# Attention block: weights' lower parts on GpSimd in halves, one reciprocal for two rows, output halves stored apart and added on reload

## The chip, the cores and the metric

The kernel runs on one core of one Trainium2 chip. The metric is the device time of one execution in microseconds. Five engines work side by side, each through its own instruction stream in a fixed order: TensorE (PE; its weight loads are PEld), VectorE (DVE), ScalarE (ACT), GpSimd (POOL) and SyncE (SP), which issues nearly all DMA transfers. An engine that waits for an input holds up everything behind it in its own stream.

## The reference

One decoder layer, 1024 tokens, width 1024. The input is normalised and multiplied by `w_in`. From the columns of that product come a forgetting attention ("fox", 8 heads of 64, causal, with a cumulated log-sigmoid bias), a sparse attention ("nsa", 8 heads of 64 in two key/value groups) and two gates. Cut to what matters here:

```python
z = h @ w_in
p = softmax(q_i k^T * SCALE + c_i - c_j)              # fox, causal
o_fox = p @ v
p_cmp, p_slc, p_win = softmax of compressed, selected, window scores
o_nsa = g0 * (p_cmp @ vc) + g1 * (p_slc @ v_sel) + g2 * (p_win @ vw)
merged = sigmoid(g_a) * (o_fox @ w_br_fox) + sigmoid(g_b) * (o_nsa @ w_br_nsa)
x = x + merged @ w_out
x = x + square(relu(rms(x) @ w_ff1)) @ w_ff2
return rms_norm(x, g_final)
```

The softmax of each row needs its exponentials, their sum (the denominator), the reciprocal of the sum, and a multiplication of the row by it.

## The kernel before

**Two-part numbers.** A matrix product is computed in three passes of rounded operands: a tensor is kept as an upper part (`hi`, a rounded copy) and a lower part (`lo`, the tensor less its rounded copy), and the product is hi·hi + hi·lo + lo·hi. For every weight tile of 128x1024, `wsplit` makes the upper part with a cast on ScalarE (L206, `wh_...`) and the lower part with one subtraction on VectorE (L207, `wl_...`). Names: `fq`, `fk`, `fv` and `nq`, `nk`, `nv` are the projections of the two attentions, `kc`, `vc`, `w1kc`, `w1vc` belong to the compressed keys and values, `g_0` to `g_7` are the gates' weights, `brf` and `brn` the two branch projections after the attentions.

**Stages of the trace.** Start and first projections (0 to 90 us), fox attention (90 to about 330), nsa attention (about 330 to 830), the nsa branch and `w_out` (830 to 960), the two feed-forward stages (960 to 1576).

**Order of the work.** `attend` writes the attention units out in turn. A unit is a pair of 128-row query blocks; for nsa it covers two heads. Between the attention's steps it puts steps of a feed: projections for later units, the gates, and at the end of the nsa stage the fox branch `brf`. The feed's pieces fill TensorE while the softmax runs on the other engines. A scheduler then fixes each engine's order from modelled times; attention steps have priority, so a feed step that is not ready in the model stands further back in TensorE's order.

**An attention unit.** Scores `sf`, `sn` are made on TensorE into three PSUM buffers; VectorE adds bias or mask and takes the minimum (L825); ScalarE takes the exponential with the sum as a by-product (L838, `denf`, `denn`); VectorE takes the reciprocal (L840, `rdf`, `rdn`); GpSimd multiplies the row (L841). Names end in the row block (0 to 7) and for nsa in `c`, `s` or `w`: compressed, selected, window; tile `pn` holds selected probabilities, `wn` compressed and window ones. TensorE transposes 128x128 blocks of a row into one of two PSUM buffers (`ptf`, `ptn`, L160); ScalarE casts them (L865 and L855) and VectorE subtracts for the lower part (the same lines); TensorE multiplies the transposed chunk with the values into `accs` (L157).

**Output of a unit.** `accs` holds, on 64 partitions, the product with the values' upper part, and on the other 64 that with the lower part. `finish` copies one half on ScalarE (L876), adds the other on VectorE (L877), each 64x256, and stores the sum to `of_d` or `on_d` in HBM. Two nsa units (`KEEP`) write straight to the tile `on`.

**Reload.** `load_of` brings the fox outputs back in eight pieces: a DMA into a buffer of the ring `vt` (L1386, `orof`), a cast on ScalarE (L1387) and a subtraction on GpSimd (L1388) into the tiles `of`. The ring `vt` has three buffers in the nsa stage (`VTN`), and is used too by the gates (`sg`: tanh on ScalarE, L786, scale on GpSimd, L787, store) and by six of the eight feature blocks of the fox branch (`msf`). `load_of` stands in the feed between the first and the second token halves of the last three gates (`g_5_0`, `g_6_0`, `g_7_0`, then the reload, then `g_5_1`, `g_6_1`, `g_7_1`), and before `brf`. The projections and gates share two PSUM buffers (`Pj`): a gate's buffer is free when its tanh has run. `load_on` does the same for the nsa outputs, placed inside the fox branch.

## Time and profile before

| | |
|---|---|
| three timed runs | 1580.92, 1578.37, 1581.56 us (median 1580.92) |
| span of the profiled execution, first to last instruction | 1576.0 us |
| mean granted TensorE clock | 0.999 |
| PE busy | 1560.9 us (99%), 7952 instructions |
| DVE busy | 1099.8 us (70%), 2434 instructions |
| ACT busy | 859.6 us (55%), 1604 instructions |
| POOL busy | 364.0 us (23%), 433 instructions |

The page gives the profiled execution only by its span; the three timed runs lie 2.4 to 5.6 us above it, which is taken as what lies around the span. Read it so: an instruction's duration runs from its start to its modelled end, and pipelined matmuls overlap, so eight matmuls of 128x512 in a row that "take 1.98 us" start their successor 1.81 us after their own start. A row of the timeline gives start, duration, engine, line, operation, output <- inputs, shape, count, and in brackets the idle time before it with what ended it.

### The profile page before, as it was taken

How to read it: one execution, taken by the hardware profiler on the slowest of the kernel's cores; microseconds unless marked ns; L12 is line 12 of the kernel's file. 1: busy time of each engine (PE TensorE's matmuls, PEld its weight loads, DVE VectorE, ACT ScalarE, POOL GpSimd, SP SyncE). 2: the span in 40 equal slices, each digit the busy share in tenths (PEclk: the TensorE clock that was granted, in tenths of full speed). 3: DMA queues.
4: the chain of work that ended last, by engine and by line, in shares of the span. 5: the costliest groups of instructions: out<-in, count | busy, mean ns of one | idle time of the engine just before them, and what ended most of it. 6: DMA issues, size and time to landing. Idle time of an engine off the chain costs nothing.

```text
span 1576.0 us, 23281 instructions
## 1 busy us (share of the span) xinstructions
PE 1560.9 (99%) x7952; PEld 1316.9 (84%) x7952; DVE 1099.8 (70%) x2434; ACT 859.6 (55%) x1604; POOL 364.0 (23%) x433
## 2 busy tenths in 40 slices
PE   8999999999999999999999999999999999999998
PEld 7888888888888888888888888888888888888886
DVE  7677768757566677548658389665556599777877
ACT  6666666646565676558543267555555644333335
POOL 1133333213332233236310000433333100000002
PEclk9999999999999999999999999999999999999999
DMA  6321212242222122224448552554444696545312
GB/s 192 77 59 49 65 49 63 90 109 64 64 74 68 34 54 74 62 68 135 156 162 299 190 167 87 194 169 155 157 148 147 224 324 217 159 145 169 112 54 107
DMA packets 165951, 196.66 MB, mean 125 GB/s; under 512 B 21497, under 2 KB 101433, under 8 KB 165825
## 3 DMA queue, kind: packets, MB, share of 16 engines
q1 hardware_dynamic: 165832, 195.18, 38.7%
q8 instruction: 63, 1.03, 0.3%
q14 instruction: 56, 0.45, 0.1%
HBM read 139.99 MB, written 55.15 MB: 124 GB/s over the span
## 4 chain that ended last, share of the span: by engine, by line
PE 94%; DVE 2%; ACT 1%; DMA 1%; SPq 1%; issue 0%; DVEq 0%; ACTq 0%
PE g L157 11%; PE fX L157 11%; PE oX L157 10%; PE accs L157 9%; PE fZ L157 6%; PE wo L157 5%; PE oZ L157 5%; PE ptn L160 4%; PE nq L157 3%; PE brn L157 3%; PE fk L157 3%; PE fv L157 3%; PE fq L157 3%; PE fW L157 2%; PE brf L157 2%; PE oW L157 2%
## 5 line engine op out<-in xcount | busy, mean ns | idle before, releaser
L157 PE MATMUL oX<-to,so 128*128 128x512 f32 x672 | 154.6, 389 | 0.0
L157 PEld LDWEIGHTS oX<-to,so 128*128 128x128 f32 x672 | 126.2, 188 | 26.2
L865 DVE TENSOR_TENSOR PTn<-ptn,PTn 128x512 fp32r<-128x512 f32 (+1 forms) x136 | 91.2, 672 | 67.8 <-ACT PTn L865 66.7
L1875 ACT CAST to<-w 128x1024 fp32r<-128x1024 f32 x48 | 48.2, 1051 | 146.8 <-PE accs L157 55.8
L865 ACT CAST PTn<-ptn 128x512 fp32r<-128x512 f32 (+1 forms) x136 | 76.6, 570 | 73.4 <-PE ptn L160 62.6
L157 PE MATMUL fX<-ht,w1h 128*128 128x512 f32 x384 | 95.0, 389 | 0.6 <-DVE ht L1581 0.6
L1713 POOL TENSOR_TENSOR ss<-w 128x512 f32<-128x512 f32 x14 | 22.4, 1602 | 309.6 <-DMA w<-in_w_ff_dram 189.0
L157 PE MATMUL accs<-PTn,Vnv 128*128 128x512 f32 (+1 forms) x304 | 92.4, 393 | 0.5 <-DVE PTn L865 0.5
L157 PEld LDWEIGHTS fX<-ht,w1h 128*128 128x128 f32 x384 | 72.0, 188 | 15.9 <-DVE ht L1581 1.0
L841 POOL TENSOR_SCALAR pf<-pf,rdf 128x896 f32<-128x896 f32 (+3 forms) x64 | 51.3, 807 | 141.9 <-DVE rdf L840 116.3
L1993 POOL TENSOR_TENSOR z<-x,gf 128x512 f32<-128x512 f32 x8 | 11.0, 1395 | 306.1 <-DVE x L1924 303.8
L157 PE MATMUL oZ<-to,so 128*128 128x512 f32 x336 | 77.6, 389 | 0.0
L157 PE MATMUL g<-hTh,wh_g 128*128 128x512 f32 (+1 forms) x288 | 76.3, 385 | 1.2 <-ACT hTh L311 1.2
L1703 DVE TENSOR_TENSOR w1l<-w,w1h 128x1024 fp32r<-128x1024 f32 (+1 forms) x32 | 34.6, 1081 | 60.4 <-ACT w1h L1702 60.4
L157 PE MATMUL g<-hTl,wh_g 128*128 128x512 f32 (+1 forms) x288 | 75.9, 384 | 0.1
L157 PEld LDWEIGHTS oZ<-to,so 128*128 128x128 f32 x336 | 63.1, 188 | 13.1
L157 PE MATMUL g<-hTh,wl_g 128*128 128x512 f32 x256 | 70.3, 396 | 0.0
L1876 DVE TENSOR_TENSOR so<-hr,so 128x1024 fp32r<-128x1024 f32 x56 | 68.0, 1236 | 0.9 <-ACT so L1875 0.9
L1875 ACT CAST so<-hr 128x1024 fp32r<-128x1024 f32 x56 | 56.7, 1049 | 18.2 <-DMA hr<-hid_d 18.1
L838 ACT ACTIVATE pf<-pf,mf 128x896 f32<-128x896 f32 (+3 forms) x64 | 49.7, 777 | 23.8 <-DVE mf L825 21.2
L1876 DVE TENSOR_TENSOR to<-w,to 128x1024 fp32r<-128x1024 f32 x48 | 56.7, 1220 | 7.7 <-ACT to L1875 7.7
L157 PEld LDWEIGHTS g<-hTh,wh_g 128*128 128x128 f32 x288 | 51.1, 188 | 10.8 <-ACT hTh L311 2.1
(511 smaller groups left out, 4248.8 us busy)
## 6 DMA issues: line engine op xcount, KB each, us to landing
w<-in_w_ff_dram SPq DMA_DIRECT2D x62, 512.0 KB, 4.4
hr<-hid_d SPq DMA_DIRECT2D x56, 512.0 KB, 4.5
wr_wo<-in_w_out_dram SPq DMA_DIRECT2D x20, 512.0 KB, 3.8
x<-in_x_dram SPq DMA_DIRECT2D x16, 512.0 KB, 8.8
wr_g<-in_w_in_dram SPq DMA_DIRECT2D x16, 512.0 KB, 3.8
hid_d<-h22s SPq DMA_DIRECT2D x32, 256.0 KB, 2.2
hid_d<-s2s SPq DMA_DIRECT2D x32, 256.0 KB, 2.0
hid_d<-s3h SPq DMA_DIRECT2D x32, 256.0 KB, 2.3
```

What stands on the lines that cost most here:

```text
L157: self.last = self.nc.tensor.matmul(*a, **k)
L160: self.last = self.nc.tensor.transpose(*a, **k)
L838: nc.scalar.activation(p, p, AF.Exp, bias=nm, scale=-1.0, accum_out=den)
L841: self.scaled = nc.gpsimd.tensor_scalar(p, p, r, 1.0 if gate is None else gate, op0=OP.mult, op1=OP.mult).ins
L865: two = nc.scalar.copy(th, src).ins, nc.vector.tensor_sub(tl, src, th.bitcast(F32)).ins
L1703: nc.vector.tensor_sub(lo, src, hi.bitcast(F32))
L1713: e.tensor_add(p[:, 4:8], b[:, 0:4], b[:, 4:8])
L1875: nc.scalar.copy(o[:, 0, s], src)
L1876: nc.vector.tensor_sub(o[:, 1, s], src, o[:, 0, s].bitcast(F32))
L1993: nc.gpsimd.tensor_mul(y[:, c], x[:, c], gf[:, c])
```

## The change

Four edits, all in the two attention stages:

1. `wsplit`: while `lo_pool` is set (both `attend` calls and what stands between them), the lower part of a weight tile is made by GpSimd in two subtractions of 128x512 instead of one of 128x1024 on VectorE. By the engines' orders these are 46 weight tiles: 92 instructions on GpSimd in place of 46 on VectorE. The `brn` and `wo` weights stay on VectorE.
2. `softmax`: the denominators of two rows stand side by side and share one reciprocal. In a fox unit these are the unit's two rows, and both rows' multiplications stand behind the second row's exponential; in nsa they are the compressed and the selected part of one row. 256 reciprocals become 160.
3. `finish`: `accs` is copied as it is by one ScalarE instruction (128x256 or 128x512) and both halves are stored apart, so VectorE's additions go and 46 stores become 92. The two `KEEP` units stay as they were.
4. `load_o`: each of the 16 reloads fetches two halves into two buffers of the ring `vt` and adds them on GpSimd (128x512) before the cast and the subtraction.

```diff
-            nc.vector.tensor_sub(lo, raw, hi.bitcast(F32))
+            if self.lo_pool:
+                k = shape[0] // 2
+                for c in (slice(0, k), slice(k, 2 * k)):
+                    nc.gpsimd.tensor_sub(lo[:, c], raw[:, c], hi[:, c].bitcast(F32))
+            else:
+                nc.vector.tensor_sub(lo, raw, hi.bitcast(F32))
...
-    def softmax(self, p, nm, name, gate=None):
+    def softmax(self, rows, name, box=None, last=True):
...
-        nc.scalar.activation(p, p, AF.Exp, bias=nm, scale=-1.0, accum_out=den)
-        r = sp.tile([P, 1], F32, tag="rd", bufs=8, name=f"rd{name}")
-        nc.vector.reciprocal(r, den)
-        self.scaled = nc.gpsimd.tensor_scalar(p, p, r, 1.0 if gate is None else gate,
-                                              op0=OP.mult, op1=OP.mult).ins
+        for p, nm, gate in rows:
+            n = len(box["rows"])
+            nc.scalar.activation(p, p, AF.Exp, bias=nm, scale=-1.0, accum_out=box["den"][:, n:n + 1])
+            box["rows"].append((p, gate))
+        if not last:
+            return
+        n = len(box["rows"])
+        r = sp.tile([P, 2], F32, tag="rd", bufs=8, name=f"rd{name}")
+        nc.vector.reciprocal(r[:, 0:n], box["den"][:, 0:n])
+        for x, (p, gate) in enumerate(box["rows"]):
+            self.scaled = nc.gpsimd.tensor_scalar(p, p, r[:, x:x + 1], 1.0 if gate is None else gate,
+                                                  op0=OP.mult, op1=OP.mult).ins
...
-        t = self.att.tile([P, 256], F32, tag="ot", bufs=3, name=f"ot{name}")
+        m = len(js)
+        t = self.att.tile([P, m, 256], F32, tag="ot", bufs=4 - m, name=f"ot{name}")
+        if dst is not None:
+            nc.scalar.copy(t, pa[:, 0:m * 256].rearrange("p (j q) -> p j q", j=m))
+            for x in range(2):
+                nc.sync.dma_start(dst[x].rearrange("(j d) t -> d j t", j=m)[:, :, q0:q0 + 256],
+                                  t[64 * x:64 * x + 64])
+            return
...
-                raw = self.att.tile([P, H], F32, tag="vt", bufs=self.VT, name=f"or{name}{half}{j}")
-                nc.sync.dma_start(raw[:, c], src[j * P:(j + 1) * P, half * H + c.start:half * H + c.stop])
+                raw, low = (self.att.tile([P, H], F32, tag="vt", bufs=self.VT, name=f"or{name}{half}{j}{x}")
+                            for x in range(2))
+                for x, d in enumerate((raw, low)):
+                    nc.sync.dma_start(d[:, c], src[x, j * P:(j + 1) * P, half * H + c.start:half * H + c.stop])
+                nc.gpsimd.tensor_add(raw[:, c], raw[:, c], low[:, c])
```

The edits also move instructions far from their own lines, since the scheduler orders by modelled times. Three places follow. In the changed kernel L841 is L858, L787 is L793, L207 is L210 on GpSimd, L1387 and L1388 are L1414 and L1415, and the new addition is L1413; a row ending in x2 stands for two such instructions.

GpSimd's order at the start of the fox reload, in the nsa stage. Before:

```order
L1388 TENSOR_TENSOR of_8660<-orof_8662,of_8660 128x512
L1388 TENSOR_TENSOR of_8661<-orof_8666,of_8661 128x512
L841 TENSOR_SCALAR wn_6_8647<-wn_6_8647,rdn_6c,gate 128x64
L1388 TENSOR_TENSOR of_8660<-orof_8670,of_8660 128x512
L1388 TENSOR_TENSOR of_8661<-orof_8674,of_8661 128x512
L841 TENSOR_SCALAR pn_6_8650<-pn_6_8650,rdn_6s,gate 128x896
L1388 TENSOR_TENSOR of_8660<-orof_8678,of_8660 128x512
```

And now:

```order
L1413 TENSOR_TENSOR orof_8429<-orof_8429,orof_8430 128x512
L1415 TENSOR_TENSOR of_8427<-orof_8429,of_8427 128x512
L1413 TENSOR_TENSOR orof_8436<-orof_8436,orof_8437 128x512
L858 TENSOR_SCALAR wn_6_8414<-wn_6_8414,rdn_6s,gate 128x64
L858 TENSOR_SCALAR pn_6_8417<-pn_6_8417,rdn_6s,gate 128x896
L1415 TENSOR_TENSOR of_8428<-orof_8436,of_8428 128x512
L1413 TENSOR_TENSOR orof_8443<-orof_8443,orof_8444 128x512
L210 TENSOR_TENSOR wl_brf_8354<-wr_brf_8112,wh_brf_8353 128x512 x2
L858 TENSOR_SCALAR wn_6_8414<-wn_6_8414,rdn_6w,gate 128x640
L1415 TENSOR_TENSOR of_8427<-orof_8443,of_8427 128x512
L1413 TENSOR_TENSOR orof_8450<-orof_8450,orof_8451 128x512
```

Each piece of the reload now has two GpSimd instructions, and the branch weights' lower parts stand between them, ahead of the probabilities' multiplications.

GpSimd's order at the end of the same reload, where the first of the late gates is scaled (`sg_51`). Before:

```order
L1388 TENSOR_TENSOR of_8660<-orof_8686,of_8660 128x512
L841 TENSOR_SCALAR wn_7_8759<-wn_7_8759,rdn_7c,gate 128x64
L1388 TENSOR_TENSOR of_8661<-orof_8690,of_8661 128x512
L787 TENSOR_SCALAR sg_51_8830<-sg_51_8830 128x512
L841 TENSOR_SCALAR pn_7_8762<-pn_7_8762,rdn_7s,gate 128x1024
L787 TENSOR_SCALAR sg_61_8950<-sg_61_8950 128x512
```

And now:

```order
L858 TENSOR_SCALAR wn_3_8972<-wn_3_8972,rdn_3s,gate 128x64
L858 TENSOR_SCALAR pn_3_8975<-pn_3_8975,rdn_3s,gate 128x512
L858 TENSOR_SCALAR wn_3_8972<-wn_3_8972,rdn_3w,gate 128x512
L1413 TENSOR_TENSOR orof_8471<-orof_8471,orof_8472 128x512
L1415 TENSOR_TENSOR of_8428<-orof_8464,of_8428 128x512
L1415 TENSOR_TENSOR of_8427<-orof_8471,of_8427 128x512
L1413 TENSOR_TENSOR orof_8478<-orof_8478,orof_8479 128x512
L793 TENSOR_SCALAR sg_51_8615<-sg_51_8615 128x512
L1415 TENSOR_TENSOR of_8428<-orof_8478,of_8428 128x512
L793 TENSOR_SCALAR sg_61_8729<-sg_61_8729 128x512
```

Before, the reload ended among the multiplications of rows 6 and 7 of the first head; now it ends behind those of rows 2 and 3 of the next unit's second head. The buffer that `sg_51` takes in the ring `vt` is the one that the last subtraction but one (`of_8427<-orof_8471`) lets go.

TensorE's order from the gate `g_6_1` to the gate `g_7_1`. Before, at the border of the two:

```order
L157 MATMUL sn_7w_8807<-kw_6913,Qnq_0_7235 128x320 x2
L157 MATMUL g_6_1_8836<-hTh_84,wh_g_6_8332 128x512 x4
L157 MATMUL sn_6_0_8817<-ks_6912,Qnq_1_7236 128x512 x2
L157 MATMUL g_7_1_8964<-hTh_84,wl_g_7_8453 128x512 x8
L157 MATMUL g_7_1_8964<-hTl_85,wh_g_7_8452 128x512
L160 MATMUL ptn_0_3_8887<-idn,pn_1_8386 128x128
```

And now, the last rows of `g_6_1` and the first of `g_7_1` with what stands next to them:

```order
L157 MATMUL accs<-PTn_0_8485,Vnv_6322 128x512 x2
L157 MATMUL g_6_1_8621<-hTh_84,wh_g_6_8107 128x512
L157 MATMUL sn_6_0_8602<-ks_6741,Qnq_1_7054 128x512 x2
L160 MATMUL ptn_0_3_8669<-idn,pn_1_8162 128x128
...
L157 MATMUL accs<-PTn_3_9007,Vnv_6322 128x512
L160 MATMUL ptn_3_11_9055<-idn,wn_6_8606 128x128
L160 MATMUL ptn_3_11_9055<-idn,wn_7_8663 128x128
L157 MATMUL g_7_1_8741<-hTh_84,wl_g_7_8226 128x512 x8
```

Before, two score matmuls stood between the gates. Now 123 instructions stand there, all of the attention and none of the feed: 29 matmuls with 512 moving columns, 6 with 448, 10 with 384, 18 with 320, 8 with 256, and 52 transposes. The fox branch `brf`, whose first rows stood among the next unit's scores before, follows `g_7_1` as it did.

More of the change, by code (lines that the diff above doesn't have):

```diff
@@ L214 @@
     wcap = 3
+    lo_pool = False
     VT, VTN = 2, 3
@@ L833, in scores @@
             steps.append((2 * max(e - c, 256) / 2.4, lambda pj=pj: piece(pj)))
-    def softmax(self, p, nm, name, gate=None):
+    def softmax(self, rows, name, box=None, last=True):
         nc, sp = self.nc, self.small
-        den = sp.tile([P, 1], F32, tag="den", bufs=8, name=f"den{name}")
-        nc.scalar.activation(p, p, AF.Exp, bias=nm, scale=-1.0, accum_out=den)
-        r = sp.tile([P, 1], F32, tag="rd", bufs=8, name=f"rd{name}")
-        nc.vector.reciprocal(r, den)
-        self.scaled = nc.gpsimd.tensor_scalar(p, p, r, 1.0 if gate is None else gate,
-                                              op0=OP.mult, op1=OP.mult).ins
+        box = {} if box is None else box
+        if not box:
+            box["den"] = sp.tile([P, 2], F32, tag="den", bufs=8, name=f"den{name}")
+            box["rows"] = []
+        for p, nm, gate in rows:
[10 more added lines that the diff above has]
+                                                  op0=OP.mult, op1=OP.mult).ins
     def turn(self, blocks, dst, name, fold=None):
@@ L870, in finish @@
         nc = self.nc
-        t = self.att.tile([P, 256], F32, tag="ot", bufs=3, name=f"ot{name}")
+        m = len(js)
[6 more added lines that the diff above has]
+            return
+        t = t[:, 0]
         for n, j in enumerate(js):
@@ L878, in finish @@
         rows = slice(64 * js[0], 64 * js[-1] + 64)
-        if dst is not None:
-            nc.sync.dma_start(dst[:, q0:q0 + 256], t[rows])
-            return
         on, c = self.on[q0 // H], slice(q0 % H, q0 % H + 256)
@@ L947, in fox_unit @@
         j = h % 2
-        rows, s1 = {}, []
+        rows, s1, dens = {}, [], {}
         def load_bias():
@@ L981, in fox_unit @@
             self.scores(s1, qf, kf, i, 0, spans, nm,
-                        lambda m, x=x, n=n, nm=nm: self.softmax(rows[x][:, 0:n], m[0], nm))
+                        lambda m, x=x, n=n, nm=nm: self.softmax([(rows[x][:, 0:n], m[0], None)], nm, dens, x == 1))
         blk = lambda x, t: rows[x][:, t * P:(t + 1) * P]
@@ L999, in fox_unit @@
                                   (v(a + 1), b[1][:, 256:384], b[2][:, 256:384], lambda acc: acc[:, P:256])]))
-        dst = self.of_d[h * HD:(h + 1) * HD, :]
+        dst = [self.of_d[x, h * HD:(h + 1) * HD, :] for x in range(2)]
         s2 = self.pv(chunks, f"f{h}_{g}", lambda acc: self.finish(acc, (j,), dst, g * 256, f"f{h}_{g}"))
@@ L1055, in slc_done @@
                 def slc_done(m, j=j, x=x, n=n, nm=nm, gt=gt):
-                    self.softmax(rows["w", j, x][:, 0:CPAD], m["c"], nm + "c", gt(0))
-                    self.softmax(rows["p", j, x][:, 0:n], m["s"], nm + "s", gt(1))
+                    self.softmax([(rows["w", j, x][:, 0:CPAD], m["c"], gt(0)),
+                                  (rows["p", j, x][:, 0:n], m["s"], gt(1))], nm + "s")
                 q = lambda j=j: qf(j)
@@ L1064, in nsa_unit @@
                             lambda m, j=j, x=x, nw=nw, nm=nm, gt=gt: self.softmax(
-                                rows["w", j, x][:, CPAD:CPAD + nw], m["w"], nm + "w", gt(2)))
+                                [(rows["w", j, x][:, CPAD:CPAD + nw], m["w"], gt(2))], nm + "w"))
         sb = lambda j, x, t: rows["p", j, x][:, t * P:(t + 1) * P]
@@ L1098, in nsa_unit @@
                                    (vw(b), two(bx[1][:, 256:H]), two(bx[2][:, 256:H]), of(1))]))
-        dst = None if (p, g) in self.KEEP else self.on_d[p * P:(p + 1) * P, :]
+        dst = None if (p, g) in self.KEEP else [self.on_d[x, p * P:(p + 1) * P, :] for x in range(2)]
         s2 = self.pv(chunks, f"n{p}_{g}", lambda acc: self.finish(acc, (0, 1), dst, g * 256, f"n{p}_{g}"), True)
@@ L1209, in attention @@
         nc, tc, a = self.nc, self.tc, self.a
-        self.of_d = self.dp.tile([512, T], F32, name="of_d")
-        self.on_d = self.dp.tile([512, T], F32, name="on_d")
+        self.of_d = self.dp.tile([2, 512, T], F32, name="of_d")
+        self.on_d = self.dp.tile([2, 512, T], F32, name="on_d")
         self.ga_d = self.dp.tile([D, T], F32, name="ga_d")
@@ L1342, in attention @@
                                                  lambda o=o: o["v"]), dl[h // 2]))
+            self.lo_pool = True
             self.DM = {k: 6000.0 for k in dl[2:3]}
@@ L1362, in attention @@
             run(f2.steps[k:])
+        self.lo_pool = False
     NGATE = 7
```

## The prediction, on record before the result was known

> **What bounds the kernel now.** I read the page's shares first, then the chain of waits, then busy time by stage. From the page, shares by engine and the head of the chain:
>
> ```profile
> span 1576.0 us, 23281 instructions
> PE 1560.9 (99%) x7952; PEld 1316.9 (84%) x7952; DVE 1099.8 (70%) x2434; ACT 859.6 (55%) x1604; POOL 364.0 (23%) x433
> ```
>
> TensorE is busy for all but 15 us. The change removes no matmul, so nothing can come out much below 1560 us. The table by stretches (columns: stretch, length, then PE, PEld, DVE, ACT, POOL busy with counts, clock, DMA share, GB/s), for the fox and the nsa attention:
>
> ```profile
> 90.00:330.00 240.00, 239.43 (x1426) 209.52 (x1425) 177.99 (x510) 152.68 (x311) 75.96 (x85) 1.00 0.24 66
> 330.00:830.00 500.00, 498.96 (x2658) 422.87 (x2657) 317.78 (x1081) 291.75 (x685) 168.79 (x250) 1.00 0.28 85
> ```
>
> Here lies everything the change touches, and TensorE's visible idle time is 0.57 + 1.04 = 1.61 us. VectorE, at 74% and 64%, is off the path, so freeing it is worth little by itself. The same table in 10 us steps shows where the 1.04 us are:
>
> ```profile
> 710.00:720.00 10.00, 10.00 (x55) 8.57 (x54) 7.20 (x24) 7.88 (x18) 7.16 (x7) 1.00 0.51 146
> 720.00:730.00 10.00, 10.00 (x56) 8.54 (x55) 8.92 (x31) 8.02 (x16) 7.86 (x10) 1.00 0.43 146
> 730.00:740.00 10.00, 9.87 (x53) 8.34 (x52) 7.47 (x35) 6.97 (x17) 4.15 (x5) 1.00 0.50 157
> 740.00:750.00 10.00, 9.48 (x53) 7.58 (x53) 9.21 (x44) 8.34 (x27) 7.99 (x13) 1.00 0.28 94
> 760.00:770.00 10.00, 9.61 (x53) 7.57 (x52) 6.81 (x20) 5.15 (x11) 2.95 (x3) 1.00 0.58 197
> ```
>
> All of it is in 730 to 770, just behind the fox reload, and there three engines are at 80 to 90% together. This is the one place without slack, and the change puts its most work there.
>
> **The change part by part.** Durations, from the groups with shapes apart (busy, mean ns | idle before):
>
> ```profile
> L207 DVE TENSOR_TENSOR wl_g<-wr_g,wh_g 128x1024 fp32r<-128x1024 f32 x16 | 19.9, 1242 | 5.2 <-ACT wh_g L206 5.2
> L1388 POOL TENSOR_TENSOR of<-orof,of 128x512 fp32r<-128x512 f32 x8 | 10.3, 1291 | 2.5 <-ACT of L1387 1.8 <-DMA orof<-of_d 0.7
> L877 DVE TENSOR_TENSOR otn<-accs,otn 64x256 f32<-64x256 f32 x32 | 13.5, 421 | 6.6 <-ACT otn L876 6.0
> L840 DVE RECIPROCAL rdf<-denf 128x1 f32<-128x1 f32 x64 | 10.0, 159 | 11.5 <-ACT pf L838 11.2
> ```
>
> *Totals.* VectorE loses 46 x 1.24 = 57 us of lower parts, 60 x 0.42 = 25 us of additions and 96 x 0.16 = 15 us of reciprocals: 97 us. GpSimd gains 92 x 1.29 = 119 us (the subtraction of L1388 has the halves' shape) and 16 additions of that price, 14 of them full, some 20 us: 139 on 245 us in the two stages, 52% of 740. ScalarE's copies get fewer and wider; the 46 added stores stand on SP, behind which only other transfers wait. These are averages, so each is worth what it does at its place.
>
> *Lower parts.* Most weights are split tens of microseconds ahead of their matmuls, and that work hides a GpSimd price twice that of VectorE. The tight border is where nsa's first projection begins:
>
> ```profile
> 327.41 1.22 DVE L207 TENSOR_TENSOR wl_nq<-wr_nq,wh_nq 128x1024 fp32r<-128x1024 f32 x1
> 328.68 2.12 PE L157 MATMUL nq<-hTh,wl_nq 128*128 128x512 f32 x8
> ```
>
> VectorE ends 0.05 us ahead of TensorE. On GpSimd the first half would end at the same time and the second 1.3 later, while the second half's matmuls start some 0.9 later (four at 0.23): a cost of 0.4 us, or 1.3 more if GpSimd is one half behind. I take 0.5, bounds 0 to 2.
>
> *Relief elsewhere.* A lower part on VectorE can be blocked by GpSimd. From the timeline:
>
> ```profile
> 115.95 1.28 POOL L942 TENSOR_TENSOR cm<-cb,cmask 128x512 f32<-128x512 f32 x1
> 116.04 2.27 DVE L207 TENSOR_TENSOR wl_fv<-wr_fv,wh_fv 128x1024 fp32r<-128x1024 f32 x1 [1.28 <-ACT wh_fv L206]
> ```
>
> The usual 1.24 became 2.27 behind an instruction that had 1.19 left. Such collisions go, since VectorE no longer subtracts weights there. What TensorE can gain is its idle time: 1.61 us less what lies in the stretches above, 0.6, and perhaps as much again hidden inside modelled matmul ends. I take a gain of 1, bounds 0 to 4. The Trainium skill, "SBUF — State Buffer", section "Who interferes with whom", states that a VectorE instruction with two SBUF inputs and a GpSimd instruction that reads SBUF exclude each other for the whole instruction, whichever came first; the 2.27 agrees (1.19 + 1.24 = 2.43). By that rule the move removes the conflict rather than moving it, which speaks for the rival "faster" below; the sum goes by TensorE's idle time.
>
> *Reciprocals and output halves.* A fox row's multiplication now waits for the second row's exponential, at most this:
>
> ```profile
> L838 ACT ACTIVATE pf<-pf,mf 128x1024 f32<-128x1024 f32 x8 | 9.2, 1152 | 5.7 <-DVE mf L825 5.6
> ```
>
> GpSimd's next work is that row anyway. I cost both edits at nothing, hidden by the transposes of the unit before; without that cover it is under 0.2 us a unit, and 32 units at a tenth of that are inside the bounds above.
>
> *The fox reload.* Here the order decides. `g_7_1` needs a `Pj` buffer, held until the tanh of `g_5_1` has run; that tanh needs a `vt` buffer, which comes free with GpSimd's last subtraction but one. Before, the feed stayed close. Timeline rows of GpSimd and TensorE:
>
> ```profile
> 707.04 0.62 POOL L787 TENSOR_SCALAR sg<-sg 128x512 f32<-128x512 f32 x1 [6.74 <-ACT sg L786]
> 707.63 1.28 POOL L1388 TENSOR_TENSOR of<-orof,of 128x512 fp32r<-128x512 f32 x1
> 722.96 1.29 POOL L1388 TENSOR_TENSOR of<-orof,of 128x512 fp32r<-128x512 f32 x1
> 723.35 1.08 PE L157 MATMUL g<-hTh,wh_g 128*128 128x512 f32 x4
> 724.74 1.98 PE L157 MATMUL g<-hTh,wl_g 128*128 128x512 f32 x8
> 726.55 0.39 PE L157 MATMUL g<-hTl,wh_g 128*128 128x512 f32 x1
> 738.53 1.20 POOL L841 TENSOR_SCALAR pn<-pn,rdn_7s,gate 128x1024 f32<-128x1024 f32 x1 [3.29 <-DVE rdn_7s L840]
> ```
>
> The reload ended at 724.25 and `g_7_1` began at 724.74 (723.35 is the last of `g_6_1`; eight matmuls take 1.81, 0.226 each). Now 123 attention instructions stand between the two. Prices of the narrower ones, from the timeline (two with 320 columns, of which the next row starts 0.30 later) and the chain of waits (four with 256, four transposes):
>
> ```profile
> 719.27 0.46 PE L157 MATMUL sn<-ks,Qnq 128*128 128x320 f32 x2
> 719.73 0.47 PE accs L157 x4
> 720.20 0.44 PE ptn L160 x4
> ```
>
> At 0.226 (512 columns), 0.15 (320), 0.115 (256), 0.11 a transpose, and between these 0.20 (448) and 0.17 (384), they are 6.6 + 1.2 + 1.7 + 2.7 + 0.9 + 5.7 = 18.8 us. TensorE without a wait would reach `g_7_1` at 724.7 + 18.7 = 743.4.
>
> GpSimd's work from the reload's first addition to the subtraction that frees the buffer, counted in its new order: 14 reload instructions at 1.29 (18.1), two branch weights in four halves (5.2), and the multiplications of rows 6 and 7 of two heads and rows 2 and 3 of two:
>
> ```profile
> L841 POOL TENSOR_SCALAR pn<-pn,rdn_7s,gate 128x1024 f32<-128x1024 f32 x8 | 9.6, 1200 | 20.2 <-DVE rdn_7s L840 20.2
> L841 POOL TENSOR_SCALAR pn<-pn,rdn_6s,gate 128x896 f32<-128x896 f32 x8 | 8.7, 1093 | 16.2 <-DVE rdn_6s L840 16.2
> L841 POOL TENSOR_SCALAR wn<-wn,rdn_6w,gate 128x640 f32<-128x640 f32 x8 | 7.0, 878 | 6.4 <-DVE rdn_6w L840 6.4
> L841 POOL TENSOR_SCALAR pn<-pn,rdn_3s,gate 128x512 f32<-128x512 f32 x8 | 6.2, 771 | 7.0 <-DVE rdn_3s L840 5.6 <-DVE rdn_3w L840 1.4
> L841 POOL TENSOR_SCALAR pn<-pn,rdn_2s,gate 128x384 f32<-128x384 f32 x8 | 5.3, 662 | 2.0 <-DVE rdn_2s L840 2.0
> L841 POOL TENSOR_SCALAR wn<-wn,rdn_6c,gate 128x64 f32<-128x64 f32 x8 | 3.1, 393 | 19.3 <-DVE rdn_6c L840 19.3
> ```
>
> Two each of 1.20 and 1.09, four of 0.88 (both window parts), four of 0.77, four of 0.66 and eight of 0.39 to 0.53: 2.4 + 2.2 + 3.5 + 3.1 + 2.7 + 3.4 = 17.3. Together 40.5 us. From 707.6 it ends at 748.1 even if GpSimd never waits, and the tanh adds 0.6:
>
> ```profile
> L786 ACT ACTIVATE sg<-g 128x512 f32<-128x512 f32 x32 | 19.0, 595 | 16.6 <-PE g L157 12.9 <-issue 2.0 <-POOL pn L841 1.0
> ```
>
> So `g_7_1` can begin at 748.7. TensorE loses 748.7 - 743.4 = 5.3 us at least.
>
> GpSimd will wait, though: for the second pair of halves, since a pair needs two of three ring buffers, and between addition and subtraction stands ScalarE's cast. The load (KB, us to landing) and the cast:
>
> ```profile
> orof<-of_d SPq DMA_DIRECT2D x8, 256.0 KB, 2.6
> ```
>
> ```profile
> L1387 ACT CAST of<-orof 128x512 fp32r<-128x512 f32 x8 | 4.9, 622 | 1.7 <-DMA orof<-of_d 1.6
> ```
>
> The second pair's load starts when the first addition has read its buffer (707.6 + 1.3) and lands at 711.5, while the first subtraction ends at 710.8 (1.3, 0.6, 1.3 after 707.6): 0.7 us lost. And it waits for exponentials, since nothing but attention runs and ScalarE and VectorE have more to do per microsecond of TensorE than at 740 to 750, where 9.21 and 8.34 of 10 were busy. Before, the row at 738.53 had a 3.29 us wait. I add 3 of the 0 to 5 that this can be: 8 us, bounds 5 to 10. Late next are `g_7_1` and `brf`; with them the feed is back among the attention, and TensorE has no slack to win the time back. In exchange the 1.04 us of waits in 730 to 770 are replaced by this one: 1 off.
>
> *Sum against the profiled span:* 1576.0 + 8 - 1 - 1 + 0.5 = 1582.5, some 6 us more. Against the runs' median, 4.9 above that span, 1580.92 + 6 = 1587.
>
> **The rivals.**
>
> *No change.* GpSimd's waits overlap its backlog, so TensorE loses the bare 5.3, and relief (4 us) with the 1 us pays it back: 0 to +1, 1581 us. For it: VectorE is nearly idle of weights in the stretch. Against: 1.61 us of visible idle time in 740.
>
> *Faster.* TensorE's matmuls hide waits in their modelled ends. If GpSimd's chain starts or ends earlier than counted, because the stretch before it runs faster without VectorE's weights, the stretch costs under 2 and relief brings its 4 and the 1: 3 less, about 1577 to 1578. It decides if the reload ends before 745. Against it stands the count of 40.5 us.
>
> *The second reload and the border too.* `on` now needs eight pairs through the same ring and GpSimd. Its last subtraction started at 806.2, by the group of that line, and its first reader at 812.55, by the timeline:
>
> ```profile
> L1388 POOL TENSOR_TENSOR on<-oron,on x8: 740/1288/1298, 760.7 to 806.2; 128x512 fp32r<-128x512 f32 x6, 128x256 fp32r<-128x256 f32 x2
> ```
>
> ```profile
> 812.55 0.84 PE L157 MATMUL brn<-on,wl_brn 128*128 128x512 f32 x3
> ```
>
> That leaves 5.6 us; with pairs at some 5 us each (2.6 load, 1.29, 0.62 cast, 1.29 less overlap) and the last two pieces behind the unit that writes them, it could cost up to 4 us, the border 2: +12, 1592 us. It decides once a pair waits for a third buffer held by `msf`.
>
> **How the numbers follow.** The forecast (TensorE starved behind `g_6_1`, 1583 to 1591) gets 0.50, the larger loss 0.14, no change 0.21, faster 0.15. A measurement of this kernel can tell 0.2% or 3.2 us from nothing, so same is 1577.8 to 1584.1. The lower edge of the forecast touches it: slower 0.63, same 0.22, faster 0.15. The range leaves out the ends of both outer cases: 1577.5 to 1593; the forecast's own is 1583 to 1591.
>
> **What would show it.** Right: TensorE's busy time in 725 to 760 falls by 5 to 10 us, with GpSimd's chain (L1413, L1415, L858) nearly gapless there and `g_7_1` starting at 749 to 754; VectorE some 97 us and GpSimd 139 us off their former totals; PE's instruction count equal. Step by step wrong: a wait of TensorE of over 1 us at 325 to 335 (border), or before `brn` (second reload), or fox waits on `pf` rows (shared reciprocal). The forecast falls if `g_7_1` starts before 746, or if TensorE's gaps elsewhere shrink by more than 4 us.

## The result

The changed kernel took **1597.60 us** (median of 4 runs, 1596.00 to 1598.45) against 1580.19 us for the kernel before (median of 4, 1578.37 to 1581.56): 1.0114 times the time, 95% interval 1.0102 to 1.0126, or 17.4 us more. The direction was the forecast one. The size was not: 1587.0 was forecast and the range ended at 1593.

From the page of the kernel after, the span and the shares by engine:

```profile
span 1596.3 us, 23152 instructions
PE 1568.3 (98%) x7952; PEld 1319.3 (83%) x7952; DVE 1019.3 (64%) x2232; ACT 851.7 (53%) x1590; POOL 493.7 (31%) x541
```

TensorE runs the same 7952 matmuls. VectorE lost 80 us of busy time (97 forecast) and GpSimd gained 130 (139), and TensorE's idle time went from 15.1 to 28.0 us. To see where, three matmuls serve as milestones: the first score matmul of fox, the first query projection of nsa, and the first matmul on nsa's output. From the view of one tile each, kernel after (count, shortest/median/longest ns, then first and last start in us):

```profile
L157 PE MATMUL sf<-Kf,Qfq x192: 220/342/478, 68.6 to 324.9; 128*128 128x512 f32 x48, 128*128 128x384 f32 x48, 128*128 128x448 f32 x32, 128*128 128x320 f32 x32
L157 PE MATMUL nq<-hTh,wl_nq x64: 387/393/478, 334.6 to 598.9; 128*128 128x512 f32 x64
L157 PE MATMUL brn<-on,wl_brn x64: 389/389/398, 832.0 to 882.4; 128*128 128x512 f32 x64
```

The first score matmul of the kernel before, from the same view:

```profile
L157 PE MATMUL sf<-Kf,Qfq x192: 220/358/497, 67.9 to 319.1; 128*128 128x512 f32 x48, 128*128 128x384 f32 x48, 128*128 128x448 f32 x32, 128*128 128x320 f32 x32
```

With the prediction's 328.68 and 812.55 for the other two, the **fox stretch** (68.6 to 334.6) takes 266.0 us where it took 260.8, 5.2 more, and the **nsa stretch** (334.6 to 832.0) 497.4 where it took 483.9, 13.5 more. The rest of the span differs by 1.6. All experiments below are read by these two stretches of one profiled execution, and by their medians.

The windows of the two kernels over the same places (stretch, length, then busy us and count of PE, PEld, DVE, ACT, POOL, granted clock, DMA share, GB/s), before:

```profile
90.00:345.00 255.00, 254.43 (x1504) 222.05 (x1503) 182.24 (x518) 155.29 (x318) 76.96 (x89) 1.00 0.25 68
345.00:700.00 355.00, 355.00 (x1901) 302.63 (x1900) 229.03 (x823) 217.79 (x523) 120.28 (x190) 1.00 0.21 62
700.00:765.00 65.00, 64.35 (x343) 53.57 (x342) 43.30 (x143) 40.57 (x91) 30.84 (x38) 1.00 0.42 137
765.00:840.00 75.00, 74.61 (x384) 62.44 (x383) 46.01 (x115) 32.54 (x68) 16.68 (x19) 1.00 0.47 153
```

and after:

```profile
90.00:345.00 255.00, 249.14 (x1474) 217.35 (x1473) 144.85 (x441) 152.69 (x316) 124.96 (x128) 1.00 0.29 79
345.00:700.00 355.00, 355.00 (x1898) 302.99 (x1897) 193.97 (x729) 212.97 (x511) 165.54 (x229) 1.00 0.24 66
700.00:765.00 65.00, 60.69 (x321) 47.87 (x320) 35.84 (x131) 39.72 (x92) 44.14 (x49) 1.00 0.35 108
765.00:840.00 75.00, 71.02 (x350) 58.51 (x349) 37.19 (x92) 29.35 (x59) 31.38 (x31) 0.95 0.54 174
```

TensorE's idle time rises by 5.3 us in fox, by nothing in the long middle of nsa, by 3.7 at the fox reload and by 3.6 at the second reload, where the clock also falls. The forecast's first sign, TensorE's busy time in 725 to 760, fell by 3.7 us (34.35 to 30.69), not by 5 to 10. What TensorE waits for, from the view of the waits of the kernel after (total us, times, longest):

```profile
PE brf L157 <- DVE msf L1464: 3.5, 2, 2.8
PE ptf L160 <- DVE PTf L882: 3.4, 4, 1.1
PE accs L157 <- DVE PTn L882: 2.3, 3, 1.1
PE ptf L160 <- POOL pf L858: 1.6, 3, 0.7
```

Two of the four are `ptf`, the transposes of fox's probability rows, of which the prediction expected nothing.

**The fox reload.** Timeline of GpSimd, ScalarE and TensorE after: the reload's first addition, the end of `g_6_1`, the last subtraction but one, the tanh that was waiting for its buffer, and `g_7_1`:

```profile
714.19 1.28 POOL L1413 TENSOR_TENSOR orof<-orof,orof 128x512 f32<-128x512 f32 x1
731.01 0.39 PE L157 MATMUL g<-hTh,wh_g 128*128 128x512 f32 x1
755.65 1.28 POOL L1415 TENSOR_TENSOR of<-orof,of 128x512 fp32r<-128x512 f32 x1 [0.40 <-ACT of L1414]
757.01 0.61 ACT L792 ACTIVATE sg<-g 128x512 f32<-128x512 f32 x1
758.82 2.09 PE L157 MATMUL g<-hTh,wl_g 128*128 128x512 f32 x8
```

The 5 us of it in which TensorE has most idle time:

```profile
745.00:750.00 5.00, 3.19 (x17) 2.15 (x18) 3.25 (x10) 4.54 (x13) 5.00 (x9) 1.00 0.36 105
```

GpSimd is busy for the whole of every 5 us from 725 to 755, while TensorE is at 3.19 to 5.00. GpSimd's chain from the first addition to the end of the subtraction that frees the buffer, 714.19 to 756.93, lasts 42.7 us, 39.1 of work and 3.6 of waits; the forecast counted 40.5 and 3. Everything here lies 6.56 us later than before (714.19 against 707.63), so TensorE without a wait would have come to `g_7_1` at 743.4 + 6.56 = 750.0. It came at 758.8: 8.8 us lost, where 8 were forecast (the forecast's 749 to 754 lie, moved by the same 6.56, at 755.6 to 760.6). Counted from the end of `g_6_1`, the 123 instructions take 27.6 us for 18.8 us of work, which is the same 8.8.

The wait is another than the forecast named, though. The tanh had ended at 757.62, and TensorE was at attention instructions without a gap from then to 758.82, so it did not wait for the gate's buffer. Its waits in 725 to 760, 3.9 us in all, lie among those attention instructions, and each is put down to VectorE (`mn`, the minimum of a score row, and `PTn`, the conversion of a transposed chunk); about half of the 8.8 does not show as idle time. The profile's chain of waits runs there through VectorE and ScalarE, the engines of the softmax, and not through GpSimd. Four of its rows, in order of time (L831 is the bias and minimum, L850 the exponential):

```profile
733.22 0.42 DVE pn L831
740.79 0.71 ACT pn L850 x2
746.65 0.72 ACT pn L850 x2
749.84 0.50 PE accs L157
```

So GpSimd's chain would have held `g_7_1` until 757.6, and the attention, with no feed between its steps, held it until 758.8.

**The second reload.** The chain of waits after, in order of time:

```profile
804.61 2.61 DMA oron<-on_d
807.43 1.30 POOL oron L1413
808.76 0.63 ACT on L1414
809.46 1.28 POOL on L1415
810.76 3.00 DMA msf<-ga_d
813.88 0.70 DVE msf L1464
814.63 5.49 PE brf L157 x12
```

A pair of output halves, its addition, cast and subtraction stand ahead of the load of `msf`, which takes the ring buffer that the subtraction frees; the last `brf` matmuls wait for `msf`. They also run slowly, as the windows show:

```profile
812.50:813.50 1.00, 0.00 (x0) 0.00 (x0) 0.00 (x0) 0.00 (x0) 1.00 (x1) 1.00 0.30 115
813.50:814.60 1.10, 0.00 (x0) 0.00 (x0) 0.69 (x1) 0.89 (x2) 0.37 (x2) 0.52 0.00 0
815.00:817.50 2.50, 2.50 (x7) 1.93 (x7) 1.82 (x3) 0.30 (x1) 0.69 (x1) 0.50 0.74 221
820.00:825.00 5.00, 5.00 (x27) 4.05 (x26) 2.17 (x4) 1.27 (x3) 0.00 (x0) 0.96 0.56 183
```

TensorE stood still for 2.81 us, up to 814.63; 1.7 us into this wait the granted clock fell to half, and the matmuls behind it ran at 0.50: twelve matmuls in 5.49 us instead of 12 x 0.226 = 2.7. With the 2.8 us of waiting, that makes some 5.6 us at this one place.

### The profile page after: what moved, and what is told of

It reads as the page before. It is cut to its first block, busy times and chain, and to the rows that moved or that the text cites. A ratio compares the mean times of both kernels' runs of the same rounds, so it can differ in the third digit from the quotient of the medians.

```text
span 1596.3 us, 23152 instructions
## 1 busy us (share of the span) xinstructions
PE 1568.3 (98%) x7952; PEld 1319.3 (83%) x7952; DVE 1019.3 (64%) x2232; ACT 851.7 (53%) x1590; POOL 493.7 (31%) x541
## 4 chain that ended last, share of the span: by engine, by line
PE 87%; DVE 3%; ACT 2%; DMA 2%; issue 1%; POOL 1%; ACTq 0%; DVEq 0%; POOLq 0%; SPq 0%
PE fX L157 11%; PE g L157 10%; PE oX L157 10%; PE accs L157 8%; PE fZ L157 5%; PE wo L157 5%; PE oZ L157 5%; PE ptn L160 4%; PE nq L157 3%; PE brn L157 3%; PE fW L157 2%; PE oW L157 2%; PE sn L157 2%; PE fv L157 2%; PE brf L157 2%; PE fq L157 2%
## 5 line engine op out<-in xcount | busy, mean ns | idle before, releaser
L882 DVE TENSOR_TENSOR PTf<-ptf,PTf 128x512 fp32r<-128x512 f32 (+1 forms) x80 | 49.3, 633 | 41.6 <-ACT PTf L882 41.6
L858 POOL TENSOR_SCALAR pf<-pf,rdf 128x896 f32<-128x896 f32 (+3 forms) x64 | 48.5, 773 | 85.7 <-DVE rdf L856 73.2
L850 ACT ACTIVATE pf<-pf,mf 128x896 f32<-128x896 f32 (+3 forms) x64 | 49.6, 777 | 25.6 <-DVE mf L831 24.3
```

The lines of the kernel that those rows point to most:

```text
L850: nc.scalar.activation(p, p, AF.Exp, bias=nm, scale=-1.0, accum_out=box["den"][:, n:n + 1])
L858: self.scaled = nc.gpsimd.tensor_scalar(p, p, r[:, x:x + 1], 1.0 if gate is None else gate, op0=OP.mult, op1=OP.mult).ins
L882: two = nc.scalar.copy(th, src).ins, nc.vector.tensor_sub(tl, src, th.bitcast(F32)).ins
```

## The experiments

The forecast's theory was that GpSimd's own work in the fox reload costs nearly everything. The rivals: the ring of three buffers, which a pair holds two of; the softmax edits and the lower parts in fox; and the addition as a link of its own in the reload, wherever it runs. The first four kernels take the change apart.

**Only the lower parts on GpSimd.**

```diff
 # before, plus only:
+            if self.lo_pool:
+                k = shape[0] // 2
+                for c in (slice(0, k), slice(k, 2 * k)):
+                    nc.gpsimd.tensor_sub(lo[:, c], raw[:, c], hi[:, c].bitcast(F32))
+        self.lo_pool = True     # ahead of the fox attention; False again behind nsa
```

> The kernel before with one part of the change: the lower parts of the 46 weight tiles on GpSimd in halves; reciprocals, output and reload as before. Theory A (three separate places: GpSimd's weight halves stand ahead of the multiplications in the fox stage; the doubled reload starves TensorE at 725 to 760 and again at 800 to 830): slower by 5 to 8 us, of which 4 to 6 lie in 90 to 340 and 0 to 2 in 725 to 760, nothing in 800 to 830. Theory B (the shared reciprocal makes the first fox row wait, the weights are harmless): within 2 us of the kernel before. My prediction's step (relief of VectorE is a gain): 0 to 2 us faster in 90 to 700.

Measured: 1581.56 us against 1579.65, ratio 1.0011 [1.0002, 1.0021]. Fox +2.3, nsa +0.1.

**Only the shared reciprocal** (the change's `softmax` and its calls, the rest as before).

> The kernel before with the shared reciprocal alone. Theory A: within 2 us of the kernel before in every stretch. Theory B: slower by 4 to 6 us, all in 90 to 340, with TensorE waiting for multiplied fox rows (pf).

Measured: 1586.23 us, 1.0044 [1.0029, 1.0058]. Fox +4.8, nsa +3.5.

**Only the output halves** (the change's finish and reload, the rest as before).

> The kernel before with output halves stored apart and added by GpSimd on reload, alone. Theory A: slower by 8 to 12 us: TensorE's idle time in 725 to 760 up by 4 to 6 us, in 800 to 830 by 4 to 7 us with the clock falling below 1.0 there, the fox stage within 1 us. Theory B (all of the loss in the nsa stage needs weights and reload on GpSimd together): 0 to 4 us slower, reload hidden.

Measured: 1596.54 us, 1.0107 [1.0091, 1.0122]. Fox +0.5, nsa +15.3.

**The change with the lower parts on VectorE.**

```diff
-        self.lo_pool = True
```

> The changed kernel with the weights' lower parts put back on VectorE as one subtraction of 128x1024. Theory A: 5 to 8 us of the 17 to 18 come back, nearly all in 90 to 340 and some 2 us in 725 to 760; the loss in 800 to 830 stays. Theory B: the loss of the fox stage stays, and 2 to 4 us come back at 725 to 760.

Measured: 1601.01 us, 1.0133 [1.0117, 1.0148]. Fox +2.2, nsa +21.8: slower than the change itself, by 3.4 us of the medians. So the two stretches have different causes. Fox belongs to the softmax edit and the lower parts, nsa nearly all to the output halves, and in nsa the halves cost more when VectorE also has the weights. GpSimd's load alone cannot be what sets the reload, since here GpSimd had less to do. Alone the three parts cost 1.9 + 6.6 + 16.9 = 25.4 us, together 17.4 to 18: they don't add up. Nor do they in fox, where the shared reciprocal costs 4.8 alone and 2.2 beside the halves; why was not looked into.

**Is it the ring?** The second half goes into a tile that the reload has anyway, the one its subtraction writes later, so a piece holds one ring buffer as before:

```diff
-                raw, low = (self.att.tile([P, H], F32, tag="vt", bufs=self.VT, name=f"or{name}{half}{j}{x}")
-                            for x in range(2))
+                raw = self.att.tile([P, H], F32, tag="vt", bufs=self.VT, name=f"or{name}{half}{j}")
+                low = t[:, 4 + j].bitcast(F32)
```

> The changed kernel, but the second half of each reload is fetched into the place where its lower part will lie in the tile of or on, so that a reload takes one buffer of the ring vt instead of two; every instruction of GpSimd, ScalarE and the DMA queues stays. Theory ring (three buffers for pairs make the reload slow, and hold the gates and msf): 8 to 12 us faster than the changed kernel, 6 to 7 us of it in 800 to 830 where the clock stays at 1.0, and 2 to 5 in 725 to 760. Theory GpSimd (its 16 added instructions and their place in its order are the cost): within 3 us of the changed kernel.

Measured: 1598.63 us against 1579.17, 1.0118 [1.0100, 1.0136]. Fox +5.6, nsa +15.6. The ring alone is worth nothing: TensorE's waits for `msf` in 700 to 845 go from 3.5 us to 0.2, but others stand in their place, for `PTn` (4.1) and for rows that GpSimd multiplies (3.0).

**The change without the output halves** (lower parts and shared reciprocals).

> The kernel before with the lower parts on GpSimd and the shared reciprocal, without the halves. If the parts add up: 1.9 plus 6.6, 8 to 9 us slower than before. If the lower parts on GpSimd repay what the reciprocal loses in the fox stage, as they seem to repay something in the change as a whole (4.6 slower than it with them back on VectorE): 3 to 6 us slower.

Measured: 1584.09 us, 1.0030 [1.0020, 1.0040]. Fox +5.8, nsa -0.5. It has all of the fox loss, and none of nsa's.

**The shared reciprocal in one stage alone.** In nsa (fox calls `softmax` a row at a time), and in fox (nsa calls it for each part); the lines against the kernel with the shared reciprocal in both:

```diff
 # in nsa only: fox gives no box
-  ... self.softmax([(rows[x][:, 0:n], m[0], None)], nm, dens, x == 1)
+  ... self.softmax([(rows[x][:, 0:n], m[0], None)], nm)
 # in fox only: nsa's two parts apart
-  self.softmax([(rows["w", j, x][:, 0:CPAD], m["c"], gt(0)),
-                (rows["p", j, x][:, 0:n], m["s"], gt(1))], nm + "s")
+  self.softmax([(rows["w", j, x][:, 0:CPAD], m["c"], gt(0))], nm + "c")
+  self.softmax([(rows["p", j, x][:, 0:n], m["s"], gt(1))], nm + "s")
```

> The kernel before with the shared reciprocal in the nsa attention alone (compressed and selected part of one row). Theory wait (a fox row waits for the other row of its unit; in nsa both parts belong to one row and come one behind the other): within 2 us of before in the fox stage and at most 2 slower in 725 to 760. Theory scheduler (any change of the modelled times reshuffles the orders and costs): 3 to 6 us slower.

> The kernel before with the shared reciprocal in the fox attention alone. Theory wait: 4 to 6 us slower, all of it in 60 to 340, with stalls of TensorE of 1.3 us between transposes of pf rows, where three chunks of transposes stand in a row with two PSUM buffers. Theory scheduler: half of the 6.6 us of the shared reciprocal, spread over both stages.

Measured: in nsa 1580.62 us, 1.0007 [0.9997, 1.0016], not told apart from before; in fox 1584.97 us, 1.0033 [1.0021, 1.0045], fox +4.9. The timeline of TensorE shows why. Before, seven transposes of fox rows stood ahead of the feed's matmuls of `fk` and four right behind:

```profile
116.10 0.95 PE L160 MATMUL ptf<-idn,pf 128*128 128x128 f32 x7
117.24 2.10 PE L157 MATMUL fk<-hTh,wl_fk 128*128 128x512 f32 x8
119.30 0.66 PE L160 MATMUL ptf<-idn,pf 128*128 128x128 f32 x4
```

With the reciprocal shared in fox, two stand ahead of them (not shown), and ten behind:

```profile
117.40 2.10 PE L157 MATMUL fk<-hTh,wl_fk 128*128 128x512 f32 x8
119.34 0.82 PE L160 MATMUL ptf<-idn,pf 128*128 128x128 f32 x6
121.29 0.66 PE L160 MATMUL ptf<-idn,pf 128*128 128x128 f32 x4 [1.13 <-DVE PTf L876]
```

A PSUM buffer takes four of them and there are two. The two ahead and the first six behind fill both, and TensorE waits 1.13 us until VectorE has converted one; four such waits in fox make 3.7 us. The first row's multiplication waits for the second row's exponential, and in the changed order its transposes stand later. GpSimd's timelines, before and with the reciprocal shared in fox, show how much later (the second line holds four multiplications, the first row's first):

```profile
109.69 1.02 POOL L841 TENSOR_SCALAR pf<-pf,rdf 128x896 f32<-128x896 f32 x1 [10.74 <-DVE rdf L840]
114.69 3.97 POOL L852 TENSOR_SCALAR pf<-pf,rdf 128x896 f32<-128x896 f32 x4 [11.60 <-DVE rdf L850]
```

That is 5.0 us, since the two rows' exponentials do not stand back to back: the second starts 4.1 us after the first (108.97 and 113.08).

**Moving the addition to VectorE, with pairs still in the ring** (`nc.vector.tensor_add` for `nc.gpsimd.tensor_add`), and the same with one ring buffer a piece.

> The changed kernel with the additions of the reload on VectorE instead of GpSimd; pairs of halves still take two buffers of the ring vt. Theory GpSimd (it is busy without a gap from 725 to 755 and holds the multiplications back): 4 to 7 us faster than the changed kernel, all in 725 to 800, and the loss in 800 to 830 (pairs in the ring) stays. Theory joint (ring and GpSimd each alone are enough to starve TensorE): within 3 us of the changed kernel.

> The changed kernel with both: additions on VectorE, and the second half of each reload fetched into the target tile, so that a reload takes one ring buffer. By both theories the two losses behind the reloads go: 10 to 13 us faster than the changed kernel, some 1585 to 1588, with the fox stage's 6 us left, and TensorE busy for over 39 of 40 us in 725 to 765. If the stores or the wide copy of finish cost something themselves: under 7 us faster.

Measured, against 1579.97: 1604.73 us, 1.0156 [1.0142, 1.0170], and 1596.30 us, 1.0104 [1.0090, 1.0118]. The first is the slowest of all kernels here, the second at the change's level (1585 to 1588 was expected), though its addition takes 0.69 us instead of 1.29. Timelines of VectorE and TensorE of the second show what VectorE pays for it:

```profile
718.90 0.69 DVE L1413 TENSOR_TENSOR orof<-orof,of 128x512 f32<-128x512 f32 x1 [4.86 <-DMA orof<-of_d]
720.25 0.50 PE L157 MATMUL accs<-PTn,Vnv 128*128 128x512 f32 x1 [2.07 <-DVE PTn L882]
```

An addition that is next on VectorE and whose data are still on the way holds back, for 4.86 us, the conversions of the attention behind it, and TensorE waits for one of them. The first of the two is 8.4 us worse, most of it in one place. By its timeline of TensorE, 61 attention instructions without any feed between them stand between the gates `g_6_1` and `g_7_1`, and take 21.1 us for 9.7 us of work by the prediction's prices: 11.4 lost. In the second kernel 21 stand there, and 3.7 us are lost.

**Lower parts on GpSimd from the first nsa unit on** (the flag set behind fox's steps), and the best of all parts together: that, and the halves added on VectorE with one ring buffer, reciprocals as before.

> The kernel before with the lower parts on GpSimd only from the first nsa unit on (gates, nsa projections of later units, brf), all else as before. The loss of the lower parts alone was in the fox stage (3.7 us of TensorE's time between 90 and 345), and their gain of 0.7 us in 725 to 800: 0 to 2 us faster than the kernel before. If weights on GpSimd also cost in nsa: 0 to 2 us slower.

> The best of the parts: lower parts on GpSimd from the first nsa unit on, output halves stored apart with the additions of the reload on VectorE and one ring buffer a reload, reciprocals as before. If only the reload's place in GpSimd and the ring cost anything: 0 to 3 us faster than the kernel before. If the halves keep a cost of their own: 1 to 4 us slower.

Measured: 1578.61 us, 0.9993 [0.9984, 1.0002], and 1585.84 us, 1.0040 [1.0027, 1.0052]. The first has the lowest median of all kernels, but is not told apart from before; the second is still 5.9 us slower. No version here beats the kernel before.

**The addition left out**, and then the second half not fetched either. Both start from the kernel with one ring buffer a piece; both leave out half of each output in the reload.

```diff
 # first
-                nc.gpsimd.tensor_add(raw[:, c], raw[:, c], low[:, c])
 # second, besides
-                low = t[:, 4 + j].bitcast(F32)
-                for x, d in enumerate((raw, low)):
-                    nc.sync.dma_start(d[:, c], src[x, j * P:(j + 1) * P, half * H + c.start:half * H + c.stop])
+                nc.sync.dma_start(raw[:, c], src[0, j * P:(j + 1) * P, half * H + c.start:half * H + c.stop])
```

> The changed kernel with the second half fetched into the target tile as in e5_target, and the addition of the two halves left out (so the attention outputs lack the product with the values' lower part; both transfers, cast and subtraction stay). Theory addition (the added instruction is an extra link of each reload in the order of an engine that also serves the softmax): the losses in 725 to 835 nearly go, 8 to 12 us faster than e5_target, some 1587 to 1590. Theory transfers (twice as many reloads, each waited for, and twice as many stores): within 4 us of e5_target.

> The changed kernel with the second half neither fetched nor added on reload (the attention outputs lack the product with the values' lower part); the wide copy and the two stores of finish stay. Theory finish (wide copy and split stores cost something): slower than before by more than the 4.5 us of lower parts and reciprocal together. Otherwise 1582 to 1586, and its distance to e14_noadd is the price of the second transfer.

Measured, against 1579.17 for both: 1586.95 us, 1.0049 [1.0034, 1.0064], and 1583.86 us, 1.0032 [1.0021, 1.0043]. So of the 19.5 us of the kernel they start from, leaving out the addition gives back 11.7 and the second transfer 3.1, and 4.7 remain, which is the fox loss. Finish, wide copy and split stores cost nothing that shows: the last kernel is at the level of the change without halves (1584.09). By the stretches nsa goes from +15.6 to +1.6 and to -0.1, and fox stays at +5.6 to +5.8.

The 11.7 us are not the instruction alone, since TensorE's order changes with it. Between `g_6_1` and `g_7_1` stand 63 attention instructions in the kernel that both start from (18.4 us for 10.0 of work, 8.4 lost), and 18 in the first of the two (1.9 lost). The change, the halves alone, the lower parts back on VectorE, one ring buffer, and pairs added on VectorE all have 61 to 123 there, and all lose 8.4 to 11.4 us at that place. No run held the order and left out the addition, so the instruction and the order that the scheduler makes of it were not separated.

The subtraction that ends each piece, from the view of the tile, tells the same of the fox reload (first and last start): before, after, added on VectorE with one ring buffer, addition left out, and one half alone. One fence each:

```profile
L1388 POOL TENSOR_TENSOR of<-orof,of x8: 1284/1290/1308, 707.6 to 723.0; 128x512 fp32r<-128x512 f32 x8
```

```profile
L1415 POOL TENSOR_TENSOR of<-orof,of x8: 1263/1286/1296, 717.2 to 761.0; 128x512 fp32r<-128x512 f32 x8
```

```profile
L1415 POOL TENSOR_TENSOR of<-orof,of x8: 1269/1291/1747, 720.3 to 743.8; 128x512 fp32r<-128x512 f32 x8
```

```profile
L1414 POOL TENSOR_TENSOR of<-orof,of x8: 1287/1301/1324, 721.5 to 742.8; 128x512 fp32r<-128x512 f32 x8
```

```profile
L1412 POOL TENSOR_TENSOR of<-orof,of x8: 1282/1289/1305, 714.8 to 731.6; 128x512 fp32r<-128x512 f32 x8
```

Eight subtractions spread over 15 us before, 44 after, 24 and 21 in the two between, 17 with one half. A short reload does not suffice, though: the third is nearly as short as the fourth and 8.6 us slower (16.3 over its kernel before, against 7.8), and what its rows show beside that is VectorE held up by its additions.

**Shared tiles, but a reciprocal for each fox row as soon as its sum is there** (lower parts and halves as before):

```diff
-        nc.vector.reciprocal(r[:, 0:n], box["den"][:, 0:n])
+        for x in range(n):
+            nc.vector.reciprocal(r[:, x:x + 1], box["den"][:, x:x + 1])
 # fox calls as in the change, nsa calls softmax for each part apart
```

> The kernel before with the two fox rows' denominators and reciprocals in shared tiles, as in e8_recipfox, but one reciprocal each, so that the scheduler may set the first row's reciprocal and multiplication ahead of the second row's exponential. Theory wait (the first row's multiplication is late and its transposes fall behind the next feed matmuls): back to the kernel before, within 2 us. Theory tiles (shared tiles of denominators cost by themselves): 4 to 6 us slower, as e8_recipfox.

Measured: 1579.05 us against 1579.17, 1.0001 [0.9992, 1.0011], fox +0.2, and TensorE's instructions in fox stand in the order of before. So what the shared reciprocal costs in fox is the wait of the first row for the second.

## Why the prediction was wrong, step by step

**The fox reload** was right in place and nearly in size, 8.8 us lost behind `g_6_1` for 8 forecast, and GpSimd's chain was counted well. The step that failed is the wait: "`g_7_1` needs a `Pj` buffer, held until the tanh of `g_5_1` has run". Without any other wait that would have cost 7.6 us (757.6 against 750.0), but TensorE was held by the attention ahead of `g_7_1` until 758.8, on VectorE and ScalarE. That the size fitted all the same is in part luck. On this step rested the view that GpSimd's work is the limit. GpSimd was indeed without a gap, but with less work for it, the lower parts back on VectorE, the time grew; moving the addition off it cost 7 us with pairs in the ring and gained 1 to 3 with one buffer. (With one ring buffer and the addition on GpSimd, TensorE does wait for GpSimd's rows, 3.0 us.) Without the addition 11.7 of 19.5 us went. What these runs leave standing is one instruction more between transfer and matmul, in order on an engine that the softmax needs too, together with an order of TensorE that leaves the attention without feed. The waits at VectorE's head show the first for VectorE; for GpSimd it is inferred.

**"Reciprocals and output halves … I cost both edits at nothing, hidden by the transposes of the unit before"** failed, and is the first term missing. The shared reciprocal costs 4.9 us in fox where it is the only edit. The wait was bounded by the duration of one exponential, 1.15 us; in the place shown above the row came 5.0 us later, since the second row's exponential runs about 4 us after the first. And what the wait does to the order of TensorE's work was not asked. In the changed order five fox transposes have moved from ahead of `fk` to behind it, and two PSUM buffers are then the next limit. The change itself has the same order there and the same 1.13 us. For the copies and split stores the nothing was right.

**"Most weights are split tens of microseconds ahead of their matmuls, and that work hides a GpSimd price twice that of VectorE"** is the second. It asked only who reads the lower part, and not what is queued behind it on GpSimd. From the timeline of the kernel with the lower parts alone:

```profile
157.48 2.54 POOL L210 TENSOR_TENSOR wl_fq<-wr_fq,wh_fq 128x512 fp32r<-128x512 f32 x2 [3.17 <-ACT wh_fq L206]
159.99 0.91 POOL L847 TENSOR_SCALAR pf<-pf,rdf 128x768 f32<-128x768 f32 x1
160.96 0.87 PE L160 MATMUL ptf<-idn,pf 128*128 128x128 f32 x6 [0.63 <-POOL pf L847]
```

The row's multiplication stands behind two halves of a weight that nobody needs yet, and TensorE waits 0.63 us for it. Fox lost 2.3 us in that kernel; the other 1.7 were not followed to single waits. The border stayed within its bounds of 0 to 2, at nothing: after, both halves of `wl_nq` are done in 332.77 to 335.29, the first matmul starts at 334.65, and no wait for them shows.

**"Such collisions go, since VectorE no longer subtracts weights there"** had a gain of 1 us. It is there at most in nsa (lower parts from nsa on: 1.4 us less, unclear). In fox the sign was wrong, and a collision moved. From the timeline after, a weight's halves on GpSimd and two additions of VectorE:

```profile
271.56 4.28 POOL L210 TENSOR_TENSOR wl_w1kc<-wr_w1kc,wh_w1kc 128x512 fp32r<-128x512 f32 x2
272.70 4.03 DVE L694 TENSOR_TENSOR e_kc<-e_kc,cols 128x504 f32<-128x504 f32 x2
```

The same two additions before:

```profile
269.40 2.38 DVE L688 TENSOR_TENSOR e_kc<-e_kc,cols 128x504 f32<-128x504 f32 x2
```

4.03 us for 2.38, and the two halves 4.28 for their usual 2.53. The Trainium skill, "SBUF — State Buffer", section "Who interferes with whom", says that two SBUF inputs on VectorE and a GpSimd instruction that reads SBUF exclude each other; the 1.65 and 1.75 us agree. So the rule did not speak of weights alone: other VectorE instructions with two SBUF inputs were to be looked for.

**The second reload** happened as the third rival had it, held against `msf` in one ring, but with the roles changed (`msf` waited for the pair) and with a price of 5.6 us at that place instead of up to 4, half of it by the slower clock. Its chance of 0.14 was too low: the eight pairs had to pass the same ring and engine as those of `of`, and the forecast let them pass free. The ring is where this wait shows, not what it takes to avoid the loss: with one buffer a piece the wait for `msf` is nearly gone and nsa still loses 15.6.

**The sum.** The forecast's terms were +8, -1, -1 and +0.5: 6.5 us. The span grew by 20.3: 5.2 in fox, 13.5 in nsa and 1.6 elsewhere. Of the 13.8 us between, 5.2 are fox, where nothing was forecast, 5.6 the second reload, 0.8 the fox reload's size, and 1.5 the two gains less the border, which did not come. The 0.7 left is within what single executions differ by. The forecast's base was also read wrongly: the 4.9 us between the median and the profiled span of before were taken as what lies around a span, but each run of the changed kernel lies only 1.7 to 1.8 us above its own span. The profiled execution of before was a short one, some 2.5 us below the median, and so the spans differ by 20.3 us and the medians by 17.4.

## What to carry to other kernels

When work goes to an engine with idle time, ask what stands behind it in that engine's queue and who waits for that; the average load and the first reader of the result say little. An edit that makes an early result wait for a late one is priced by when the late one comes and by what the scheduler then does with the readers, not by the duration of one instruction. A stretch of TensorE's order with attention alone ran here at the pace of the softmax engines, so look in the new order for stretches that have lost their feed. And before a term is set to nothing because something hides it, that cover has to be named in the order of the changed kernel.

## What the runs showed of the hardware

- A wait of TensorE cost twice its length: 2.81 us of waiting, and 2.8 more in the matmuls behind it. At the second reload the granted clock fell to half about 1.7 us after the last matmul had ended (it was 1.00 up to 813.5, the last matmul ended at 811.8), and stayed at 0.50 until about 820. The Trainium skill, "TensorE: Matmul & The Clock Gate", Part 1, names an idle window of about 3.4 us ahead of the half clock; here a gap of 2.8 us, after others of up to 0.5 us, was enough. With the lower parts back on VectorE the mean clock was 0.62 in 735 to 740, at the fox reload.
- An instruction that waits for a transfer at the head of VectorE stopped everything behind it for 4.86 us, though work that needed no transfer stood there.
- Two instructions each of VectorE and GpSimd took 4.03 us for 2.38 and 4.28 for 2.53 where they met: each engine was stopped by the other.
